# The modulation matrices' loads issued from GpSimd's queue in a twelve-phase transformer stack

## The chip, the cores and the metric

The kernel runs on one core of one Trainium2 chip. The metric is the device time of one execution in microseconds (us). The engines have short names in the profile: PE is TensorE, DVE is VectorE, ACT is ScalarE, POOL is GpSimd, SP is SyncE. Each has an instruction queue of its own and takes it in order: an instruction whose semaphore has not arrived holds up all that stand behind it on that engine. SPq and POOLq are the queue side of SP and POOL, on which DMAs are issued.

## What is computed

A sequence of 256 tokens by 1024 features, in float32, goes through two blocks of two layers. Each layer has three phases: a gated feed-forward net (FFN, inner width 2816), a mixer (a gated linear recurrence, a differential attention, and twice a sparse attention beside a spatial gate), and a second FFN. That makes twelve phases. Ahead of each phase the activations are normalised and modulated by rows that depend on a condition vector `c`:

```
mod = (silu(c) @ ada_w[l] + ada_b[l])            # nine rows of 1024 per layer: 3 phases x (shift, scale, gate)
h   = rmsnorm(x, g) * (1 + scale) + shift        # ahead of each phase
x   = x + gate * phase(h)                        # after each phase
```

Each row of `mod` needs a 1024x1024 slice of `ada_w`, 4 MB. These are the modulation matrices of this document.

## The kernel before

**Tiles.** Tokens are two tiles, T = 0 and 1, of 128. Every weight matrix is cut into chunks of up to four 128x512 blocks; half a chunk is loaded by one DMA of 512 KB into one of four `raw` buffers (`load_chunk`, line 194). ACT rounds it to `hi` (line 198), DVE subtracts to get `lo` (line 199), and three matmuls (`hi`, `lo` of the weight against `hi`, `lo` of the activation; two in part of the FFN) stand in for one float32 product. Eight pairs of `hi`, `lo` halves exist, so weights can be up to four chunks ahead of PE.

**Order.** The program is written out by hand as a long list: a queue of weight chunks with pieces of modulation work between them (`add_w`, `add_ada`; `ADA_SPAN` says over which chunks of a phase the pieces are spread). Every instruction has a place number in program order. `later(n)` adds n to it. A scheduler then lays out the queue of each engine from the instructions that are ready in its own reckoning, lower numbers first, and puts in the waits. On the chip each queue is then fixed.

**Modulation work.** For each of the 34 rows after the first two, `ada` takes an accumulator `acc` (two buffers) that POOL sets to zero (line 249), loads the bias `ada_b` into its first partition (SP, line 250), and then loads eight pieces `araw` of 128x1024 (512 KB each; two buffers, `ARAWS = 2`) with the DMA of line 258. DVE multiplies each by its column of silu(c) and adds it to `acc` (`accumulate`, line 265). With `ADA_LATER = 100` these accumulates have a late place number, so DVE takes them between its other work. A third `araw` can be loaded only when the first has been accumulated. When all eight are in, `row_sum` splits `acc` (lines 277, 278), adds the partitions up on PE (lines 282, 283) and writes the row; then the `acc` buffer is free.

**Norms.** At the end of each phase `residual` adds the gated output to `x` (lines 406, 407). `norm_half` then squares and sums on ACT (line 356) and makes the reciprocal root on POOL, by an add (line 358), an add (line 360) and a power (line 361). `pre` multiplies on DVE (line 379) and PE transposes the result (line 398) for the next phase's matmuls. The two tiles run three chunks apart (`LAG = 3`).

The first two rows, for phase 0, are loaded by other code (`ada_first`, line 335) into the weights' `raw` buffers; it is not touched.

Of the kernel before, what the change touches and what calls it, by code (L numbers as in the profile page):

```python
# [18 lines left out]
P = 128  # L19
D = 1024  # L20
# [61 lines left out]
class Net:  # L82
# [155 lines left out]
    def ada(self, piece):  # L238

        nc, A = self.nc, self.A  # L240
        st, q = piece
        b, l, j, kind = (st[k] for k in ("b", "l", "j", "kind"))
        sfx = "_2" if b else ""
        col = (j * 3 + kind) * D
        if q == 0:
            while len(self.row_stages) > 1:
                self.row_step()
            st["acc"] = self.t(self.tmp, [P, D], tag="acc", bufs=2)
            nc.gpsimd.memset(st["acc"], 0.0)  # L249
            nc.sync.dma_start(st["acc"][0:1, :], A["ada_b" + sfx][l:l + 1, col:col + D])  # L250
        if q == 2 and kind == 1:
            nc.sync.dma_start(self.S, A["norm_g" + sfx][l, j:j + 1, :].to_broadcast([P, D]))
        acc = st["acc"]
        for k in range(2 * q, 2 * q + 2):
            if len(self.araws) == ARAWS:
                self.accumulate()
            raw = self.araw()
            nc.sync.dma_start(raw, A["ada_w" + sfx][l][k * P:(k + 1) * P, col:col + D])
            self.araws.append((raw, k, acc, b, self.row_sum(b, l, j, kind, acc) if k == KD - 1 else None))

    def accumulate(self):
# [1161 lines left out]
def build(ctx, tc, A, which=None):  # L1423
# [15 lines left out]
    for i, (b, l, j, spec) in enumerate(ph):  # L1439
        ada = net.ada_pieces(b, l, j, 2)  # L1440
        if i + 1 < len(ph):
            b2, l2, j2, _ = ph[i + 1]
            ada += net.ada_pieces(b2, l2, j2, 1) + net.ada_pieces(b2, l2, j2, 0)
        if spec[0] == "ffn":
            cs = net.ffn_chunks(spec[1], spec[2], i == 0)
        elif spec[0] == "hgrn":
            cs = net.hgrn_chunks(A["a_w_in"][0], A["a_w_out"][0])
        elif spec[0] == "diff":
            cs = net.diff_chunks(A["b_w_in"][0], A["b_w_out"][0])
        else:  # L1450
            cs = net.nsa_chunks(A["mix_w_in_2"][l], A["proj_a_2"][l], A["proj_b_2"][l], A["w_out_2"][l])
        starts.append(len(net.chunks))
        done = 0
        for n, spec_ in enumerate(cs):
            if i == 0 and n == 3:
                net.queue.append(("f", second_half))
            if i + 1 < len(ph) and ph[i + 1][3][0] == "diff" and n == len(cs) // 2:
                net.queue.append(("f", diff_prep))
            net.add_w(*spec_)
            skip, tail = ADA_SPAN["first" if i == 0 else spec[0] if i + 1 < len(ph) else "last"]  # L1460
            want = max(0, n + 1 - skip) * len(ada) // (len(cs) - skip - tail)
            while done < min(want, len(ada)):
                net.add_ada(ada[done])
                done += 1
# [61 lines left out]
```

## Time and profile before

| what | value |
|---|---|
| time, median of 3 runs | 2245.66 us (2245.18 to 2247.92) |
| profiled execution: its own time | 2246.78 us |
| its span, first to last instruction | 2245.0 us |
| PE busy | 2201.0 us, 98% of the span |
| DVE busy | 1790.5 us, 80% |
| ACT busy | 1232.6 us, 55% |
| POOL busy | 112.8 us, 5% |
| bytes moved by DMA | 537.20 MB, mean 239 GB/s |

The span lies inside the execution's own time; 1.78 us lie around it. Busy time of PE includes matmuls that stream back to back. The difference between the span and PE's busy time, 44 us, is time in which PE did nothing.

### The profile page before, as it was taken

What the parts mean: (1) busy time and instruction counts of PE and PEld (TensorE: products, weight loads), DVE (VectorE), ACT (ScalarE), POOL (GpSimd) and SP (SyncE); (2) the same over time, 40 slices, a digit from 0 to 9 for tenths busy, and PEclk for the clock granted to TensorE, in tenths of its full rate; (3) what the DMA queues carried; (4) which work ended last, traced back from release to release, by engine and by line L of the source; (5) the groups of instructions that cost most, each with busy time, mean ns of one, the idle gap of its engine ahead of it and who ended that gap; (6) DMA issues with size and microseconds to landing.
All of it is one profiled execution on the core that took longest, in us unless ns stands there. A gap on an engine that the chain in (4) does not pass through costs nothing. (4 is left out here: it accounts for less than half of the span.)

```text
span 2245.0 us, 33267 instructions
## 1 busy us (share of the span) xinstructions
PE 2201.0 (98%) x12152; PEld 1820.6 (81%) x12152; DVE 1790.5 (80%) x2481; ACT 1232.6 (55%) x2182; POOL 112.8 (5%) x164
## 2 busy tenths in 40 slices
PE   8999999999999989999999999999999999999998
PEld 6887877888888767888888787788878878777886
DVE  7898987886878788887878778787877867887664
ACT  3664545564564586664565546466546644655653
POOL 1000101000000121000000000000000000000000
PEclk9999999999999999999999999999999999999999
DMA  9998865777877766877768787677777778755653
GB/s 299 303 310 286 286 207 185 268 256 245 265 230 263 235 225 202 286 247 253 255 224 267 232 256 227 195 254 229 262 229 255 254 247 266 244 173 179 187 171 111
DMA packets 264789, 537.20 MB, mean 239 GB/s; under 512 B 22083, under 2 KB 52619, under 8 KB 264625
## 3 DMA queue, kind: packets, MB, share of 16 engines
q1 hardware_dynamic: 264184, 534.67, 73.2%
q8 instruction: 95, 1.56, 0.3%
q14 instruction: 70, 0.57, 0.1%
q10 hardware_dynamic: 440, 0.40, 0.1%
HBM read 533.95 MB, written 1.05 MB: 238 GB/s over the span
## 5 line engine op out<-in xcount | busy, mean ns | idle before, releaser
L198 ACT ACTIVATE hi<-raw 128x1024 fp32r<-128x1024 f32 (+1 forms) x704 | 732.7, 1054 | 538.0 <-PE mm L457 329.9
L199 DVE TENSOR_TENSOR lo<-raw,hi 128x1024 fp32r<-128x1024 f32 (+1 forms) x704 | 845.1, 1214 | 221.0 <-ACT hi L198 217.2
L551 PE MATMUL mm<-hT,hi 128*128 128x512 f32 x2240 | 792.4, 398 | 0.0
L553 PE MATMUL mm<-hT,lo 128*128 128x256 f32 x2240 | 629.0, 281 | 0.0
L551 PEld LDWEIGHTS mm<-hT,hi 128*128 128x128 f32 x2240 | 420.8, 188 | 103.4
L553 PEld LDWEIGHTS mm<-hT,lo 128*128 128x128 f32 x2240 | 423.2, 189 | 1.3
L455 PE MATMUL mm<-hi,hT 128*128 128x512 f32 (+1 forms) x832 | 332.2, 399 | 1.5 <-ACT hT L385 1.1
L457 PE MATMUL mm<-hi,hT 128*128 128x512 f32 (+1 forms) x832 | 325.1, 392 | 0.5 <-DVE hT L387 0.5
L456 PE MATMUL mm<-lo,hT 128*128 128x512 f32 (+1 forms) x832 | 323.4, 389 | 0.0
L457 PE MATMUL mm<-hi,aT 128*128 128x512 f32 x704 | 278.3, 395 | 0.0
L455 PE MATMUL mm<-hi,aT 128*128 128x512 f32 x704 | 278.2, 395 | 0.0
L456 PE MATMUL mm<-lo,aT 128*128 128x512 f32 x704 | 277.8, 395 | 0.0
L265 DVE SCALAR_TENSOR_TENSOR acc<-araw,c_2s,acc 128x1024 f32<-128x1024 f32 x144 | 184.3, 1280 | 35.5 <-DMA araw<-ada_w 34.1
L455 PEld LDWEIGHTS mm<-hi,hT 128*128 128x128 f32 x832 | 156.9, 189 | 40.9 <-issue 8.6
L265 DVE SCALAR_TENSOR_TENSOR acc<-araw,cs,acc 128x1024 f32<-128x1024 f32 x128 | 163.8, 1280 | 31.2 <-DMA araw<-ada_w 30.6
L457 PEld LDWEIGHTS mm<-hi,hT 128*128 128x128 f32 x832 | 156.7, 188 | 34.5 <-DVE hT L387 1.2
L456 PEld LDWEIGHTS mm<-lo,hT 128*128 128x128 f32 x832 | 157.1, 189 | 29.9 <-issue 0.7
L456 PEld LDWEIGHTS mm<-lo,aT 128*128 128x128 f32 x704 | 132.6, 188 | 30.8
L457 PEld LDWEIGHTS mm<-hi,aT 128*128 128x128 f32 x704 | 132.6, 188 | 30.4
L455 PEld LDWEIGHTS mm<-hi,aT 128*128 128x128 f32 x704 | 132.6, 188 | 30.3
L536 ACT ACTIVATE aT<-uf 128x256 fp32r<-128x256 f32 x140 | 58.2, 416 | 92.7 <-DVE uf L534 92.7
L249 POOL MEMSET acc<- 128x1024 f32 x34 | 32.5, 956 | 1170.3 <-DVE accl L278 665.2
(287 smaller groups left out, 2182.4 us busy)
## 6 DMA issues: line engine op xcount, KB each, us to landing
araw<-ada_w SPq DMA_DIRECT2D x272, 512.0 KB
raw<-ffn_wi SPq DMA_DIRECT2D x160, 512.0 KB
raw<-ffn_w_in SPq DMA_DIRECT2D x160, 512.0 KB
raw<-ffn_wo SPq DMA_DIRECT2D x88, 512.0 KB
raw<-ffn_w_out SPq DMA_DIRECT2D x88, 512.0 KB
raw<-mix_w_in SPq DMA_DIRECT2D x64, 512.0 KB
raw<-a_w_in SPq DMA_DIRECT2D x32, 512.0 KB
raw<-b_w_in SPq DMA_DIRECT2D x24, 512.0 KB
```

Of the source, the lines that this page charges most:

```text
L198: nc.scalar.activation(hi[:, :n, :w], r, AF.Copy)
L199: nc.vector.tensor_sub(lo[:, :n, :w], r, hi[:, :n, :w].bitcast(F32))
L249: nc.gpsimd.memset(st["acc"], 0.0)
L265: self.nc.vector.scalar_tensor_tensor(acc, raw, self.cs[b][:, k:k + 1], acc, op0=OP.mult, op1=OP.add)
L455: nc.tensor.matmul(ps, lhsT=h, rhs=hi, start=start and i == 0, stop=False)
L456: nc.tensor.matmul(ps, lhsT=h, rhs=lo, start=False, stop=False)
L457: nc.tensor.matmul(ps, lhsT=l, rhs=hi, start=False, stop=stop and i == c.nk - 1)
L536: nc.scalar.activation(hi, u, AF.Copy)
L551: nc.tensor.matmul(ps[f], lhsT=c.hi(k)[:, fs], rhs=x, start=kh == 0 and k == 0, stop=False, skip_group_check=True)
L553: nc.tensor.matmul(ps[f][:, 0:256], lhsT=c.lo(k)[:, fs], rhs=x[:, 0:256], start=False, stop=kh == 1 and k == 3, skip_group_check=True)
```

## The change

The DMA that loads a piece of a modulation matrix is issued by GpSimd in place of SyncE. Source, destination, size and buffers stay as they are. The bias load (line 250), the load of the norm's gain (line 252), `ada_first` and all weight loads stay on SyncE.

```
--- before.py
+++ after.py
@@ -255,7 +255,7 @@
             if len(self.araws) == ARAWS:
                 self.accumulate()
             raw = self.araw()
-            nc.sync.dma_start(raw, A["ada_w" + sfx][l][k * P:(k + 1) * P, col:col + D])
+            nc.gpsimd.dma_start(raw, A["ada_w" + sfx][l][k * P:(k + 1) * P, col:col + D])
             self.araws.append((raw, k, acc, b, self.row_sum(b, l, j, kind, acc) if k == KD - 1 else None))
 
     def accumulate(self):
```

## Rows read from the trace of the kernel before

**Rows 1.** The page: busy time by engine; DMA share in 40 equal slices.
```profile
PE 2201.0 (98%) x12152; PEld 1820.6 (81%) x12152; DVE 1790.5 (80%) x2481; ACT 1232.6 (55%) x2182; POOL 112.8 (5%) x164
...
DMA  9998865777877766877768787677777778755653
```

**Rows 2.** Windows: stretch, length, busy us by engine (count), clock, DMA share, GB/s.
```profile
0.00:60.00 60.00, 54.11 (x207) 38.05 (x208) 42.82 (x60) 21.90 (x32) 7.30 (x16) 1.00 0.91 299
60.00:200.00 140.00, 139.51 (x718) 117.58 (x717) 125.97 (x171) 78.16 (x125) 2.46 (x3) 1.00 0.90 304
200.00:400.00 200.00, 189.94 (x1853) 162.20 (x1852) 169.95 (x213) 106.95 (x175) 19.86 (x27) 0.99 0.72 234
400.00:700.00 300.00, 299.06 (x1583) 254.41 (x1583) 243.33 (x322) 171.61 (x282) 8.12 (x11) 1.00 0.77 253
700.00:900.00 200.00, 190.25 (x909) 151.06 (x908) 163.88 (x244) 128.30 (x361) 31.53 (x39) 0.98 0.70 227
900.00:2000.00 1100.00, 1091.37 (x5697) 900.18 (x5696) 889.01 (x1264) 601.04 (x1016) 37.74 (x56) 1.00 0.76 244
...
2200.00:2245.00 45.00, 37.63 (x162) 30.09 (x161) 19.40 (x23) 13.44 (x20) 2.46 (x6) 0.94 0.28 93
```

**Rows 3.** Waits of PE: total us, times, longest us.
```profile
PE tr L398 <- DVE xs L379: 9.0, 17, 1.0
...
PE tr L398 <- ACT hi L198: 4.1, 6, 0.7
```

**Rows 4.** Waits of SP's queue, same columns.
```profile
SPq L194 <- DVE lo L199: 877.1, 484, 8.9
SPq L258 <- DVE acc L265: 234.9, 155, 6.0
...
SPq L258 <- DMA araw<-ada_w: 62.4, 43, 4.4
SPq L250 <- POOL acc L249: 49.4, 27, 3.6
```

**Rows 5.** Line 258: issue time, ns min/median/max, first and last start.
```profile
L258 SPq DMA_DIRECT2D araw<-ada_w x272: 327/341/1771, 62.6 to 1997.8; - x136
```

**Rows 6.** POOL's lines, same columns; the last is its longest instruction.
```profile
L249 POOL MEMSET acc<- x34: 952/956/962, 40.1 to 1962.6; 128x1024 f32 x34
L360 POOL TENSOR_TENSOR ss<-ss x26: 189/492/989, 15.5 to 2240.0; 128x1 f32<-128x1 f32 x26
L361 POOL TENSOR_TENSOR ss<-ss,mhalf x26: 551/570/1062, 16.2 to 2240.2; 128x1 f32<-128x1 f32 x26
L670 POOL TENSOR_TENSOR qst<-qst,mhalf x4: 1661/1664/2203, 785.4 to 829.3; 128x8 f32<-128x8 f32 x4
```

**Rows 7.** DVE's two kinds with the most work around the change, same columns.
```profile
L199 DVE TENSOR_TENSOR lo<-raw,hi x704: 741/1218/1228, 21.5 to 2223.4; 128x1024 fp32r<-128x1024 f32 x174, 128x560 fp32r<-128x560 f32 x2
L265 DVE SCALAR_TENSOR_TENSOR acc<-araw,c_2s,acc x144: 1265/1279/1286, 904.9 to 2003.0; 128x1024 f32<-128x1024 f32 x144
```

**Rows 8.** Windows of line 265 alone: stretch, length, DVE busy us (count), clock, DMA.
```profile
60.00:200.00 140.00, 38.40 (x30) 1.00 0.90 304
```

**Rows 9.** Waits of DVE: total us, times, longest us.
```profile
DVE acc L265 <- DMA araw<-ada_w: 64.7, 60, 2.8
...
DVE xs L379 <- POOL ss L361: 15.5, 22, 1.3
```

**Rows 10.** SP's queue in order of time, 0 to 130 us: start, us, issues.
```profile
62.58 0.46 SPq L258 DMA_DIRECT2D araw<-ada_w  x1
...
102.83 0.32 SPq L250 DMA_DIRECT2D acc<-ada_b  x1
```

**Rows 11.** POOL in order of time, 0 to 330 us: the second accumulator's memset.
```profile
47.10 0.96 POOL L249 MEMSET acc<- 128x1024 f32 x1 [6.00 <-PE tr L341]
```

**Rows 12.** The chain that ended last, in order of time: start, us, piece.
```profile
1969.95 3.33 DMA araw<-ada_w
...
2054.58 0.84 POOL ss L360
```

More of the change, by code (lines that the diff above doesn't have):

```diff
@@ L257, in ada @@
             raw = self.araw()
-            nc.sync.dma_start(raw, A["ada_w" + sfx][l][k * P:(k + 1) * P, col:col + D])
+            nc.gpsimd.dma_start(raw, A["ada_w" + sfx][l][k * P:(k + 1) * P, col:col + D])
             self.araws.append((raw, k, acc, b, self.row_sum(b, l, j, kind, acc) if k == KD - 1 else None))
```

## The prediction

> **What bounds the kernel now.** I read the busy times first, then the windows, the waits of PE, the queue of SP, POOL's lines, and last the chain that ended last.
>
> PE is busy 98% of the span [rows 1], and in the long stretches nearly all of it: 139.5 of 140 us from 60 to 200, 299.1 of 300 from 400 to 700, 1091.4 of 1100 from 900 to 2000 [rows 2]. There the end is set by the count of matmuls, and no load can shorten it. What is left to gain or lose is PE's idle time, 2245.0 - 2201.0 = 44 us. By stretch: 5.9 us in the first 60 (nothing to multiply yet), 10.1 from 200 to 400 and 9.8 from 700 to 900 (the linear recurrence and the differential attention, chains of small steps), 8.6 over the 1100 us from 900 to 2000, 7.4 in the tail [rows 2], and some 2 in the rest. The largest single reason that PE waits is the end of the norms: 17 waits for line 379, 9.0 us in all [rows 3]. Line 379 in turn waits for POOL's power 22 times, 15.5 us [rows 9]. So POOL, 5% busy [rows 1], stands on the path at the phase boundaries. One of its adds lies in the chain that ended last, at 2054.58, 0.84 us [rows 12].
>
> Weights are not late. SP waits 877 us at line 194, but for DVE to free a `raw` buffer [rows 4], which means that loads run ahead as far as buffers let them. PE's waits that trace to the split of weights (line 198) are 4.1 us [rows 3].
>
> **SP is relieved.** It loses 272 issues at 0.341 us [rows 5], 93 us of queue time, and the two longest waits in front of them, 234.9 us for a free `araw` and 62.4 us for a transfer [rows 4]. Behind each such wait stood weight loads. They can now go earlier, but still wait for `raw` buffers, and PE waited only 4.1 us for the split. I cost this at nothing: the cover is the lookahead of eight weight halves. The bound of the gain is that 4.1 us.
>
> The Trainium skill, "DMA: Bandwidth & Descriptors", section "Issuing engines are not separate DMA queues", says that all issuing engines feed the same 16 DMA engines, so that a second issuer only saves the first one's issue time. By that rule alone the sum would be the time before, with SP's 93 us saved off the path; the row of line 258 agrees that this time exists, and no row before can show the interleaving.
>
> **DVE may wait less.** DVE waited 64.7 us in 60 waits for an `araw` to land [rows 9], because the issue stood behind weight loads in SP. With a queue of its own a piece can be issued when its buffer is free. Little of this is on the path: the chain that ended last passes through an `araw` transfer for 3.33 us, one piece of note [rows 12]. Between nothing and 9.0 us (all of PE's waits for line 379 [rows 3], if every one came of a DVE queue held up by a late piece), I take half of the one piece that the chain shows: -1.7 us.
>
> **The start.** Before, the first piece is issued at 62.58 us, because SP has weights ahead of it [rows 10]. On POOL nothing stands in front: both `araw` buffers are empty from the start. POOL does run ahead where it can: the memset of the second accumulator runs at 47.10 us [rows 11], 56 us before SP loads that accumulator's bias at 102.83 [rows 10]. So the first two pieces may be issued in the first microseconds. They are 2 x 0.524 MB = 1.05 MB, and the first 60 us already move 299 GB/s at a DMA share of 0.91 [rows 2], so 1.05 / 0.299 = 3.5 us of other loads come later, while PE waits for its first inputs. A delay there is not won back, since PE is full from 60 us on. Below: nothing, if the scheduler leaves the two at their old place or they fall behind what PE needs. I take half, +1.7 us.
>
> **POOL's issues.** No row shows a DMA issued by POOL. From both sides: SP's issue, 0.341 us [rows 5], and POOL's longest instruction, 2.203 us [rows 6]. I take the row that it is nearest to, a POOL instruction that writes SBUF over 128 partitions and reads none, the memset at 0.956 us [rows 6]. 272 x 0.956 = 260 us, 11.6% of the span, beside the 112.8 us of now: POOL has room. What it costs is that a norm's add or power (0.492 and 0.570 us [rows 6]) finds an issue running: 0.116 x 0.956 / 2 = 0.06 us each time; with 2.203 us a piece, 0.27 x 1.1 = 0.3 us.
>
> **POOL's waits.** The waits for a free `araw` go along to POOL. An accumulate has a late place number, so POOL's head will often be a load that waits for DVE. Behind it stand the adds and powers of the norms, and the memsets; for the memset waits SP's bias load, today already 49.4 us in 27 waits [rows 4], and behind that the weights. SP met these waits late and still waited 234.9 / 155 = 1.5 us, up to 6.0 [rows 4]. Loads come every (1997.8 - 62.6) / 271 = 7.1 us [rows 5]. So a waiting load is at the head for at least 1.5 / 7.1 = 0.21 of the time. I take that share of the 17 places where PE waits for line 379 [rows 3] to lose 1.5 us each, 0.32 on average. With the 0.06 above: 17 x 0.38 = 6.4 us. Below: nothing, if the scheduled order puts each norm ahead of the loads. Above: all 17 at the 6.0 us of the longest wait, 102 us, which needs the worst order at every boundary; all 17 at the mean, 26 us, is a bound that could happen.
>
> **The sum.** 2246.8 (the profiled execution's time, 2245.0 of it span) + 6.4 + 1.7 - 1.7 = 2253.2. That execution lies 1.1 us above the median of the runs, 2245.66, so in terms of the median 2252.1: I forecast 2252 us, slower by 0.28%.
>
> **Rivals.** *No change that can be measured.* A difference under 0.2%, 4.5 us, can't be told from none: 2241.2 to 2250.2. It comes if the scheduled order of POOL puts the norms ahead of waiting loads, or the loads simply keep their old places: then 2245.7 plus or minus the two small terms, 2244 to 2249. For it: POOL is 5% busy and DVE frees buffers every few microseconds. Against it: 17 places, each of which needs only 0.26 us (4.5 / 17) to decide.
>
> *Faster.* One mechanism: DVE's in-order queue no longer stands at an accumulate whose piece is late, so the norms' multiplies and the recurrence's steps behind it go earlier. It decides from half of PE's 9.0 us on [rows 3]: 2241 to 2237, when all 9.0 go. For it: 64.7 us of such waits on an engine that is 80% busy. Against: the chain crosses only one of note.
>
> *DVE is held up by POOL.* If an instruction of POOL kept DVE's two-input operations waiting for its length, then from 60 to 200 us, where DVE is busy 126.0 of 140 [rows 2], the 30 pieces [rows 8] at 0.956 us add 28.7: 154.7 us of work in 140, 14.7 too much, for which PE would wait: 2260. Against: over 34 memsets and 26 norms on POOL, lines 199 and 265 never ran longer than 1.228 and 1.286 us against medians of 1.218 and 1.279 [rows 7], and no memset was stretched (952 to 962 ns [rows 6]). POOL's adds, which read, were (189 to 989 ns). The Trainium skill, "SBUF — State Buffer", section "SBUF: two separate sides", warns the other way round: descriptors of a DMA issued from GpSimd are made by its cores, which can't write them while DVE holds the shared port in a 2-port mode. By that the issues would be stretched rather than DVE; the trace agrees in so far as no write of POOL was stretched by these two lines; no run before shows a DMA of POOL's. The price of stretched issues is that of the bound above, 2.2 us each: 17 x (0.32 + 0.3) = 10.5, for 2256.
>
> *POOL's queue blocks at most boundaries*: 26 us of waits, 2272; behind late memsets SP's bias load and the weights go late too.
>
> **Chances and range.** The forecast, slower by 0.2 to 0.6% (2250.2 to 2260, with the stretched issues in it): 0.37. No change: 0.34. Faster: 0.18. Blocked at most boundaries, or DVE held up: 0.11, from 2260 on. So faster 0.18, same 0.34, slower 0.48. The likeliest alone lies between 2250 and 2260. The range for 8 in 10 reaches over no change into the faster case and up into the blocked one: 2239.5 to 2275.
>
> **What the profile after would show.** Right: line 258 on POOLq, 272 times, near 1 us; SP's waits at 258 gone; the first `araw` in the first 20 us, and the first matmul with weights 1 to 3 us later than before; POOL's wait list led by line 258 waiting for DVE at 265; PE's waits for line 379 grown from 9.0 to about 15 us; DVE's waits for landing pieces down from 64.7. Wrong: if the PE waits for line 379 stay, the waits in POOL's queue don't meet the norms; if PE's busy time rather than its idle time grows, the cause is none of these; if issues on POOL take several microseconds each, POOL is a bound of its own, and the time is far above the range. What would break the forecast most easily is the order that the scheduler gives all queues with a new owner for 272 DMAs: it can move every small wait of the 44 us by chance.

## The result, and the profile after

| | before | after |
|---|---|---|
| time, median (lowest to highest) | 2245.42 us (2244.57 to 2247.92) | 2282.01 us (2280.07 to 2285.76) |
| span of the profiled execution | 2245.0 us | 2279.6 us |
| PE busy, and idle in the span | 2201.0, 44.0 us | 2207.5, 72.1 us |

The ratio is 1.0158, 95% interval 1.0146 to 1.0170: 1.6% slower, 36.6 us. The direction was forecast, the size was not: 2252 us, with a range that ended at 2275. Of the 34.6 us by which the span grew, 28.1 are new idle time of PE and 6.5 new busy time.

From the page of the kernel after: busy times, one DMA queue, the chain that ended last by engine and by line, the DMA issues with their median time from issue to landing.

```profile
PE 2207.5 (97%) x12152; PEld 1821.4 (80%) x12152; DVE 1788.1 (78%) x2481; ACT 1228.7 (54%) x2184; POOL 263.6 (12%) x436
...
q0 software_dynamic: 39168, 142.62, 19.0%
...
PE mm L551 19%; PE mm L455 10%; PE mm L457 10%; PE mm L456 10%; PE mm L553 10%; DMA araw<-ada_w 8%; DVE lo L199 3%; PE tr L398 2%; ACT hi L198 2%; DVE acc L265 1%; DMA raw<-ada_w 1%; DMA raw<-ffn_wi 1%; DMA raw<-mix_w_in 1%; DVE xs L406 0%;
...
araw<-ada_w POOLq DMA_DIRECT2D x272, 512.0 KB, 4.7
```

The pieces have a queue of their own (q0), and POOL has room. Transfers of pieces are now 8% of the chain that ended last. The chain of before goes back only to 1668.85 us, the last quarter of the span, and holds one such transfer, of 3.33 us [rows 12]; over the same last part the chain of after holds 13.

Line 258 after, on POOL: ns min/median/max of one issue, first and last start.

```profile
L258 POOL DMA_DIRECT2D araw<-ada_w x272: 530/530/778, 1.7 to 2019.8; - x136
```

Waits of PE after (total us, times, longest us), to be held against [rows 3]:

```profile
PE tr L398 <- DVE w L922: 8.9, 4, 5.5
PE tr L398 <- DVE xs L379: 7.6, 15, 0.8
PE tr L398 <- DVE sst L1340: 7.5, 2, 4.6
...
PE mm L551 <- DVE gf L521: 4.4, 3, 1.6
...
PE tr L283 <- DVE accl L278: 3.5, 4, 2.6
```

The ends of the norms (line 379) cost no more than before. What grew is a handful of long waits for DVE. Line 922 turns q and k of the differential attention; PE waited for it before too, but for shorter times:

```profile
PE tr L398 <- DVE w L922: 5.3, 3, 2.2
```

Line 1340 is the softmax of the sparse attention, lines 521 and 278 belong to the FFN and to the row sums. For lines 1340 and 521 the profile before lists no wait of PE, for 278 one of 0.5 us.

Waits of DVE after, to be held against [rows 9], and below them those of POOL and of SP [rows 4]:

```profile
DVE acc L265 <- DMA araw<-ada_w: 119.0, 88, 5.5
...
DVE xs L379 <- POOL ss L361: 15.0, 22, 1.3
```
```profile
POOL araw L258 <- DVE acc L265: 812.4, 227, 12.1
```
```profile
SPq L194 <- DVE lo L199: 1224.8, 487, 18.3
...
SPq L250 <- POOL acc L249: 65.5, 30, 9.5
```

SP is rid of line 258. It waits longer than before for `raw` buffers (877.1 us before), and 65.5 us for the memset ahead of the bias load (49.4 before). POOL stands at line 258 for 812 us in SP's place. DVE's waits for landing pieces have nearly doubled, from 64.7 us in 60 waits to 119.0 in 88, where the forecast had them fall.

**Where the time went.** PE runs its 12152 instructions in both kernels, nearly all in the same order, so the start of the n-th can be compared. How much later it starts than before, gained within each stretch (times are those of before; two columns of kernels explained below):

| stretch of before, us | after | old order on POOL | norms ahead |
|---|---|---|---|
| 0 to 59, start | 3.8 | 4.3 | 5.1 |
| 59 to 220, first FFN | 9.6 | -0.9 | -0.9 |
| 220 to 767 | -0.7 | 0.2 | 2.3 |
| 767 to 897, differential attention | 6.7 | 6.7 | 2.9 |
| 897 to 1406 | 0.5 | 0.8 | 0.4 |
| 1406 to 1442, end of a sparse attention | 6.3 | 0.0 | 0.0 |
| 1442 to 1991 | 2.5 | 1.6 | 0.8 |
| 1991 to 2030, end of the second one | 4.2 | 0.0 | 0.0 |
| sum, to the last matmul | 33.1 | 12.6 | 10.6 |
| behind the last matmul | 1.6 | 1.6 | 1.6 |

The last row is the end of the program. The last matmul starts 7.8 us ahead of the end of the span where SyncE issues all loads (before, and experiment 2), and 9.3 us in the kernel after and in experiment 1. What grew is the longest of GpSimd's three drains (`DRAIN`) at line 1522, the end of the program. Before and after, ns min/median/max of one:

```profile
L1522 POOLq DRAIN  x3: 34/78/657, 2240.2 to 2244.7; - x3
L1522 POOLq DRAIN  x3: 40/102/5577, 2273.3 to 2279.4; - x3
```

**One place closely.** At the first end of a sparse attention, before and after in order of time (start, us, engine, line; in brackets the idle time before it and what ended it). Before:

```profile
1410.78 0.69 DVE L1333 TENSOR_REDUCE sst<-mm 128x2 f32<-128x512 f32 x1 [2.51 <-PE mm L1324]
...
1418.86 1.28 DVE L265 SCALAR_TENSOR_TENSOR acc<-araw,c_2s,acc 128x1024 f32<-128x1024 f32 x1
```

After:

```profile
1425.06 0.53 POOL L258 DMA_DIRECT2D araw<-ada_w  x1 [8.14 <-DVE acc L265]
...
1433.65 1.28 DVE L265 SCALAR_TENSOR_TENSOR acc<-araw,c_2s,acc 128x1024 f32<-128x1024 f32 x1 [5.53 <-DMA araw<-ada_w]
1434.85 0.68 DVE L1333 TENSOR_REDUCE sst<-mm 128x2 f32<-128x512 f32 x1
...
1440.86 1.04 PE L398 MATMUL tr<-ident,ring 128*128 128x128 f32 x4 [4.60 <-DVE sst L1340]
...
1442.26 2.08 PE L1324 MATMUL mm<-kall,qT 64*128 64x512 f32 x4
```

The piece's transfer in the chain that ended last (start, us):

```profile
1425.06 8.49 DMA araw<-ada_w
```

Before, the softmax's reduction (line 1333) runs as soon as its matmuls are done, and the accumulate follows 8 us later. After, an accumulate stands ahead of the reduction in DVE's queue. Its piece isn't there, DVE waits 5.53 us, and PE then stands 4.60 us for the softmax. Two things meet here: DVE's queue has another order, and the transfer took 8.49 us where the median is 4.7, at a DMA share of 0.98 from 1425.06 to 1433.56 us. At the median, by an estimate from these two numbers, it would have landed 3.8 us earlier. The program, sizes and buffers are the same, but with another owner for 272 DMAs the scheduler laid out the queues anew: in DVE's, 534 of 2481 places hold another kind of instruction than before, in PE's 189 of 12152. POOL's own 164 instructions keep their order.

### The profile page after: what moved, and what is told of

Same layout as the page of the kernel before. It is cut to its first block, busy times and chain, and to the rows that moved or that the text cites. A ratio compares the mean times of both kernels' runs of the same rounds, so it can differ in the third digit from the quotient of the medians.

```text
span 2279.6 us, 33403 instructions
## 1 busy us (share of the span) xinstructions
PE 2207.5 (97%) x12152; PEld 1821.4 (80%) x12152; DVE 1788.1 (78%) x2481; ACT 1228.7 (54%) x2184; POOL 263.6 (12%) x436
## 4 chain that ended last, share of the span: by engine, by line
PE 63%; DMA 10%; issue 10%; DVE 10%; ACT 4%; POOL 2%; POOLq 0%; DVEq 0%; ACTq 0%
PE mm L551 19%; PE mm L455 10%; PE mm L457 10%; PE mm L456 10%; PE mm L553 10%; DMA araw<-ada_w 8%; DVE lo L199 3%; PE tr L398 2%; ACT hi L198 2%; DVE acc L265 1%; DMA raw<-ada_w 1%; DMA raw<-ffn_wi 1%; DMA raw<-mix_w_in 1%; DVE xs L406 0%; PE tr L283 0%
## 5 line engine op out<-in xcount | busy, mean ns | idle before, releaser
L258 POOL DMA_DIRECT2D araw<-ada_w x272 | 147.2, 541 | 930.9 <-DVE acc L265 812.4
```

The costliest lines, as they stand in the source:

```text
L258: nc.gpsimd.dma_start(raw, A["ada_w" + sfx][l][k * P:(k + 1) * P, col:col + D])
```

## Experiments

In ten of the fourteen kernels an order is written down: between neighbours of a queue stands an edge that the scheduler must keep and that becomes no wait on the chip (the kernel after, and the one of experiment 8 with that order written down, both have 33403 instructions). So the order of one kernel can be run with the issuing engine of the other. The loads of line 258 are left free within their engine's queue (in experiment 5 GpSimd's whole queue, in experiment 3 all but DVE's).

```
+        row = [here[k] for k in names if k in here]
...
+        for prev, ins in zip(row, row[1:]):
+            tc.add_manual_dep(ins, prev.name,
+                              mybir.DependencyInfo(mybir.DependencyClass.NoSync, mybir.DependencyReason.DATA),
+                              reason="pin")
```

Medians below stand beside the kernel before on the same chip: 2245.4 us in experiments 1, 2 and 8, 2246.0 in 3 to 7 and 9, 2247.3 in 10.

**1. The old order, loads on GpSimd.** The kernel after, all queues in the order of before.

> GpSimd issues the 272 loads, but the order of every queue (PE, DVE, ACT, SP, POOL) is pinned to that of the kernel before; only the loads themselves are placed freely on POOL. Theory 'order' (most of the 36 us comes of where the scheduler put DVE's accumulates): 2245.4 plus the 4.5 us of the start, as the two first loads still run ahead: 2247 to 2253. Theory 'queue' (loads through POOL's queue land later or wait longer, whatever the order): 2270 to 2282, with DVE's wait for landing pieces near the 119 us of after.

2261.85 us, ratio 1.0072 (1.0057 to 1.0087): 16.4 us slower than before, and 20 faster than after. So the order is worth more than half of the loss, and the rest needs no new order. Waits of DVE and PE in it:

```profile
DVE acc L265 <- DMA araw<-ada_w: 77.1, 63, 3.2
```
```profile
PE tr L398 <- DVE xs L379: 9.4, 17, 1.0
PE tr L398 <- DVE w L922: 6.4, 2, 4.9
```

**2. The new order, loads on SyncE.** The kernel before, all queues in the order of after.

> SyncE issues all loads as in the kernel before, but the order of every queue is pinned to that of the kernel after; only the loads of line 258 are placed freely on SP. Theory 'order': slow although GpSimd issues nothing, 2268 to 2285 (the start without its 4.5 us, weights behind loads that wait a little later). Theory 'queue': 2243 to 2250.

2294.33 us, 1.0213 (1.0196 to 1.0230): the new order is slow with no DMA on GpSimd at all. Its waits of DVE and of PE:

```profile
DVE acc L265 <- DMA araw<-ada_w: 131.8, 71, 6.4
```
```profile
PE mm L551 <- DVE gf L521: 15.6, 6, 4.0
```

It is slower than after by 12 us, so issuing from GpSimd is the better of the two in this order. The two halves of the loss don't simply add, and the 49 us are not the price of the order alone. In the new order DVE takes its first accumulate before 61 us. In the kernel after, that piece is loaded from 1.75 us on. Here SyncE issues the load only at 56.97 us, behind weights; DVE waits for it and PE for DVE, so that some 8 us are lost at this one place:

```profile
56.97 8.09 SPq L258 DMA_DIRECT2D araw<-ada_w  x3
...
63.42 1.28 DVE L265 SCALAR_TENSOR_TENSOR acc<-araw,cs,acc 128x1024 f32<-128x1024 f32 x1 [6.90 <-issue]
...
65.89 0.80 PE L456 MATMUL mm<-lo,hT 128*128 128x512 f32 x1 [5.77 <-DVE lo L199]
```

**3. DVE's queue alone in the old order**, the others laid out by the scheduler.

```
+def pin(nc, tc, engines=("DVE",)):
```

> All 272 loads on POOL; only DVE's queue is pinned to the order of before, the others are laid out freely. Theory 'accumulates' (the places of line 265 in DVE's queue are what the new order lost by): 2258 to 2266, like the run with all queues pinned. Rival (the orders of PE, ACT and SP matter): 2270 to 2282.

2263.79 us, 1.0091 (1.0066 to 1.0115): with DVE's order alone 18 of the 36 us are back, nearly all that the five queues together gave. Its runs go from 2260.81 to 2272.40, so the two can't be told apart.

**4. Another place number.**

```
-ADA_LATER = 100
+ADA_LATER = 400
```

> The kernel after with ADA_LATER = 400 for 100, so that accumulates have a later place number and DVE takes them behind more of its other work. Theory 'accumulates': DVE stands less at late pieces, and the time falls by 5 to 15 us, to 2267 to 2277. Rival (the place number hardly matters, as accumulates are laid out by when the scheduler holds them to be ready): 2278 to 2286.

2281.44 us, 1.0160 (1.0144 to 1.0175). Nothing changed: DVE's queue is that of after but for two places, so a later place number doesn't bring the old order back.

**5. Six accumulates moved.** The order of after, but in DVE's queue three accumulates at each of the two ends of a sparse attention stand behind the softmax (each bracket names three accumulates and the scaling, line 1344, that they go behind).

```
+LATER = [(("I-14840", "I-14962", "I-14965"), "I-13763"), (("I-20909", "I-21123", "I-21124"), "I-19215")]
```

> After's order in every queue but for six accumulates in DVE's queue, three near 1433 us and three near 2018 us of after's trace: they stand behind the scaling of the softmax (line 1344) instead of ahead of its reduction (line 1333). Theory (DVE's accumulates were laid out ahead of work that PE waits for): PE's waits for line 1340, 4.6 and 3.7 us there, go, and so does what the two places cost against the kernel before, 6.3 and 5.2 us in steps of PE's instructions: 11 us less than after, near 2271. Rival (the pieces that DVE waits for are late anyway, and the wait only goes to another place): 2280 to 2284.

2279.84 us, 1.0153 (1.0136 to 1.0170), at the lower end of what the rival gave: the theory is refuted. The two places still lost 5.7 and 3.2 us. In order of time:

```profile
1433.66 2.60 DVE L265 SCALAR_TENSOR_TENSOR acc<-araw,c_2s,acc 128x1024 f32<-128x1024 f32 x2
...
1435.24 0.53 POOL L258 DMA_DIRECT2D araw<-ada_w  x1 [12.19 <-DVE acc L265]
...
1440.74 1.29 DVE L265 SCALAR_TENSOR_TENSOR acc<-araw,c_2s,acc 128x1024 f32<-128x1024 f32 x1 [4.48 <-DMA araw<-ada_w]
...
1443.67 0.69 DVE L1333 TENSOR_REDUCE sst<-mm 128x2 f32<-128x512 f32 x1
...
1447.96 0.63 PE L398 MATMUL tr<-ident,ring 128*128 128x128 f32 x4 [3.30 <-DVE sst L1340]
```

This shows one thing that makes a piece late. Two accumulates run, each frees a buffer, the load for the third goes out at once (1435.24) and its accumulate can start 5.5 us later. In between DVE has nothing that stands ahead of it, so it waits 4.48 us, now in front of the next softmax. Moving an accumulate back moves its successor's load back as well.

So I counted, for each accumulate, DVE's own work since the end of the accumulate two before it, the one that frees its buffer. Where that is less than a load's round trip (from the freeing accumulate's end to landing, 5.0 us by the median of after), DVE mostly waits: at 78 of the 109 such places in after. A transfer takes 3.5 to 10.3 us there, so the count is no sharp line. For the kernels with three buffers (experiment 6) it is the accumulate three before.

| kernel | under 5 us of work | DVE idle in front of accumulates, us |
|---|---|---|
| before | 84 of 270 | 64.5 |
| old order on POOL | 83 | 78.1 |
| after | 109 | 124.1 |
| new order on SP | 109 | 133.4 |
| before, 3 `araw` | 4 of 269 | 18.3 |
| after, 3 `araw` | 10 | 30.1 |

**6. A third `araw` buffer**, in both kernels, paid for with one `raw` buffer, since both don't fit.

```
-RAWS = 4
-ARAWS = 2
+RAWS = 3
+ARAWS = 3
```

> The changed kernel with three araw buffers, paid for with one of the four raw buffers. Read against before_33 alone. Theory (DVE stands at pieces that are issued too late, because a load waits in POOL's queue for one of two buffers): a third buffer lets each load be issued one piece earlier, DVE's waits for pieces fall from 119 us to half or less, and the ratio to before_33 comes down from 1.016 to 1.008 or less. Rival (what costs is the order of the queues, whatever the buffers): the ratio stays 1.013 or more.

> The kernel before with three araw and three raw buffers, the base for after_33. Both theories: slower than the kernel before by what the fourth raw buffer is worth, between nothing and 40 us; DVE's waits for pieces below the 64.7 us of before.

2308.79 us against 2268.65: before with the third buffer is 1.0101 (1.0086 to 1.0116) of before, after with it 1.0277 (1.0262 to 1.0293), so 1.8% lie between them, no less than without. DVE's waits for pieces, of after_33 and then of before_33:

```profile
DVE acc L265 <- DMA araw<-ada_w: 28.7, 21, 3.7
```
```profile
DVE acc L265 <- DMA araw<-ada_w: 16.4, 17, 3.0
```

The waits went as expected and the loss did not. This refutes late pieces as the one cause: where they are nearly gone, the change costs 40 us in a third layout. The order hurts there in other ways: PE waits 7.8 us for the softmax's scaling (line 1344), for which it waited in no place of before_33, while its waits for line 379 hardly differ (19.8 and 17.9 us).

**7. A rule in place of a written order.** Each load has an edge to the weight load that stands ahead of it in the program.

```
+            load = nc.gpsimd.dma_start(raw, A["ada_w" + sfx][l][k * P:(k + 1) * P, col:col + D])
+            self.tc.add_manual_dep(load.ins, self.weight.ins.name,
+                                   mybir.DependencyInfo(mybir.DependencyClass.NoSync, mybir.DependencyReason.DATA),
+                                   reason="behind the weights")
```

> The changed kernel with one more rule for the scheduler: a load of line 258 isn't laid out before the weight load that stands ahead of it in the program. It adds no wait on the chip, and no order is written down. Theory (half of the loss is the order that the scheduler makes when it lets GpSimd's loads run ahead of the weights): the first araw goes back behind the first weights, the start costs at most 1 us, and the time is that of the kernels with the old order, 2255 to 2266. Rival (any new order that isn't the old one costs as much): 2276 to 2290.

2308.1 us, 1.0271 (1.0249 to 1.0293), a miss for both. The first loads did go back, to 48.98 us, yet it is a fourth layout, and the slowest with two buffers. Only 67 of its accumulates have under 5 us of work, and DVE waits 74.4 us for pieces. What PE waits for most in it is the multiply of the spatial gate beside the sparse attention (lines are shifted by 3):

```profile
PE tr L401 <- DVE m L1188: 15.0, 3, 7.4
```

**8. The start.** Two kernels keep the first two loads behind the first memset of line 249, in the old order and in the new.

```
...
+            if len(self.held) < 2:
+                self.tc.keep_in_program_order(load)
+                self.held.append(load.ins.name)
```

> As the run with the order of before, and the first two loads stand on POOL behind the memset of their accumulator, which ran at 40 us in the kernel before. Theory 'start' (the two loads that run ahead cost 4.5 us): 4 to 5 us less than the run without the hold. With theory 'order' that is 2243 to 2249, no change from before; under 2241 if the free SP queue is worth something. Theory 'queue': 2265 to 2278.

> The kernel after with the order of every queue pinned to its own, except that the first two loads stand on POOL behind the memset of their accumulator. Theory 'start': the first matmul with weights returns from 30.4 to about 25.9 us, and the time falls by 4 to 5 us, to 2277 to 2278. Rival (the delay of the start is hidden by what is late anyway in the next 160 us): 2280 to 2283.

2261.32 us, 1.0071 (1.0056 to 1.0086), and 2277.81, 1.0147 (1.0125 to 1.0169). In the new order the median falls into the range of the theory, but its runs go from 2273.79 to 2283.56, and the profiled one (2281.67) was 6.2 us late at 59 us, later than without the edit, so that the start won the 4 us is not shown. In the old order nothing was won. The first matmul with weights starts at 26.60 instead of 31.32 us (25.88 before), but by 59 us PE is as late as without the edit. In order of time (lines shifted by 1 to 4):

```profile
41.40 1.33 POOL L259 DMA_DIRECT2D araw<-ada_w  x2
...
52.73 1.38 PE L402 MATMUL tr<-ident,xs 128*128 128x128 f32 x8 [2.09 <-DVE xs L383]
```

The pieces now load at 41 us, and a norm's end is late instead. At both places tried, 1.75 and 41 us, 1 MB more pushed out something that PE needs; the whole stretch moves at a DMA share of 0.91 [rows 2].

**9. Some loads back on SyncE**, in the old order: the first two, and then those of the differential attention's phase as well (24; for them `st["sp"]` is true).

```
-            nc.gpsimd.dma_start(raw, A["ada_w" + sfx][l][k * P:(k + 1) * P, col:col + D])
+            self.pieces += 1
+            (nc.sync if self.pieces <= 2 or st["sp"] else nc.gpsimd).dma_start(
+                raw, A["ada_w" + sfx][l][k * P:(k + 1) * P, col:col + D])
```

> Every queue in the order of before; the first two of the 272 loads on SP in their old place, the other 270 on POOL. Theory 'start' (two loads within the first 60 us delay inputs by 4 us, wherever POOL issues them in that time): 4 us under the run with the order of before, 2256 to 2259, and no delay at 60 us. Rival (DMA of the first 60 us is not the cause): 2260 to 2264.

> As the run with two loads on SP, and the 24 loads whose pieces belong to the differential attention's phase also on SP; 246 on POOL. Theory 'norms behind loads' (on POOL the norms of queries and keys stand behind a load that waits for DVE: 6 to 8 us lost between 780 and 900 us): 2249 to 2252. Rival (that loss is DVE waiting for pieces that land late, on either queue): 2255 to 2259.

2259.71 us, 1.0059 (1.0044 to 1.0075), and 2261.38, 1.0066 (1.0051 to 1.0081). The first misses its theory's 2259 by 0.7 us and lies 2 us under experiment 1, within what the runs scatter. At 59 us the two are 2.4 and 1.1 us late, where experiment 1 was 4.3: the delay of the start shrinks when its loads leave it, and the total hardly follows. With the attention's loads on SyncE its stretch lost 1.2 us instead of 6.7, but in that profile PE lost 3.9 us near 1030 and 4.0 near 1919, where the old order on POOL had lost nothing and 0.9. The total didn't fall: a miss. In front of the first of them (lines shifted by 2 and 3):

```profile
1007.33 0.53 POOL L260 DMA_DIRECT2D araw<-ada_w  x1 [4.94 <-DVE acc L268]
...
1014.30 1.28 DVE L268 SCALAR_TENSOR_TENSOR acc<-araw,c_2s,acc 128x1024 f32<-128x1024 f32 x1 [3.42 <-DMA araw<-ada_w]
```

A crowded accumulate again, here in an FFN, with a load that took 6.5 us to land. Why it meets PE in this execution and not in the others of the same order stays open.

**10. The norms of q and k ahead of the loads.** In the old order on POOL, at 790 us (experiment 1):

```profile
790.66 0.53 POOL L258 DMA_DIRECT2D araw<-ada_w  x1 [3.88 <-DVE acc L265]
...
791.59 1.67 POOL L670 TENSOR_TENSOR qst<-qst,mhalf 128x8 f32<-128x8 f32 x1
793.29 0.69 DVE L914 TENSOR_TENSOR w<-mm,qst 128x512 f32<-128x512 f32 x1 [2.94 <-POOL qst L670]
...
797.08 1.08 PE L398 MATMUL tr<-ident,w 128*128 128x128 f32 x4 [4.87 <-DVE w L922]
```

A load waits 3.88 us for its buffer, the norm behind it waits along, then DVE 2.94 us for the norm, then PE 4.87 us. The edit lays four loads behind the norms that follow them; the second kernel also issues the first two loads from SyncE.

```
+BEHIND = [("I-7957", "I-7729"), ("I-8023", "I-7889"), ("I-8185", "I-8148"), ("I-9273", "I-8555")]
```

> All 272 loads on GpSimd, every queue in the order of before, but in GpSimd's queue four loads of the differential attention stand behind the q/k or head norm that they stood in front of (those that in the kernel without this edit ran at 790.7, 810.0, 832.2 and 870.8 us and had waited 3.9, 3.1, 0.2 and 3.3 us for a buffer). DVE, ACT, PE and SP keep their queues. Theory (about half of what is left in the old order is norms held behind a waiting load): the stretch from 767 to 897 us of before, which lost 6.7 us in steps of PE's instructions, loses 2 or less, and the time falls from 2261.9 to 2255 to 2258. Rival (the load goes later instead, and DVE stands at its piece): 2260 to 2264.

> The same edit, and the first two loads issued by SyncE at their old place, so that the start is that of before. Theory (start and norms are the two named costs of GpSimd's issue, and the rest is small): 2250 to 2254. Rival (what is taken away at one place comes back at others, as it did when 26 loads were on SyncE): 2257 to 2263.

2262.09 us, 1.0065 (1.0053 to 1.0077), and 2255.93, 1.0046 (1.0029 to 1.0064; runs from 2252.18 to 2264.66). The same place in the first of them:

```profile
791.27 0.25 POOL L667 TENSOR_SCALAR qst<-qst 128x8 f32<-128x8 f32 x1 [1.46 <-ACT junk L906]
791.60 1.67 POOL L670 TENSOR_TENSOR qst<-qst,mhalf 128x8 f32<-128x8 f32 x1
...
793.24 0.61 POOL L258 DMA_DIRECT2D araw<-ada_w  x1
793.31 0.69 DVE L914 TENSOR_TENSOR w<-mm,qst 128x512 f32<-128x512 f32 x1 [0.41 <-PE mm L457]
...
797.09 0.63 PE L398 MATMUL tr<-ident,w 128*128 128x128 f32 x4 [1.99 <-DVE w L922]
```

The norm no longer waits for the load, PE's wait falls from 4.87 to 1.99 us, and the stretch lost 2.9 us instead of 6.7. In the medians this is 14.8 us over before instead of 16.4, within what the runs scatter and within the rival's range: the place is shown, its worth in the time is not. With both edits 8.6 us remain. In the profiled execution the steps sum to 5.4 us, of which 0.4 up to 59 us, and 1.4 more lie behind the last matmul. That is half of experiment 1's loss, and still 2 us above the range that the theory gave.

No kernel tried beats the one before.

## Why the prediction was wrong, step by step

**The step that failed** is the sum itself: it priced GpSimd's issues and waits as if each queue kept its order. The new order stood there only as what "would break the forecast most easily", without a price or a chance: the sum put it at nothing. By experiments 1 and 3 it is 18 to 20 of the 36.6 us, and by experiment 2 it costs on SyncE too. The terms that the sum did have were short as well: 6.4 us in all, where experiment 1 with the old order measured 16.4. The rows that could have warned are [rows 9] and [rows 3]: DVE already waited 64.7 us for pieces of which little met PE, so the old order held these waits off the path, and a new one need not.

**"DVE may wait less", -1.7 us**, had the wrong sign. Its size was read from a chain that covers only the last quarter of the span, so "one piece of note" told nothing of the first 1668 us. In the old order the forecast gain is there: in front of accumulates with 6 us of work or more between, DVE's idle time falls from 13.3 to 2.1 us, since their loads no longer stand behind weights. But the 101 crowded ones are bound by the round trip, and theirs rises from 51.2 to 76.0 us. By the median an accumulate's end is followed by the next load 0.30 us later on POOL and 0.03 on SP, and the issue takes 0.53 us where SP's took 0.341 [rows 5]. Together that is 0.46 us a round trip; over the 63 waits of experiment 1 it would be 29 us, an estimate from these rows that is near the 24.8 by which the crowded waits grew. In the new order 129 are that crowded, with 122.1 us.

**The start, +1.7 us**, was the right mechanism and too small. The two loads were issued at 1.75 us, and PE waited for a transfer of the first two rows' own matrices (line 340) before any weights came:

```profile
1.75 1.33 POOL L258 DMA_DIRECT2D araw<-ada_w  x2
...
14.30 2.05 PE L340 MATMUL tr<-raw,cs_rows 128*128 128x512 f32 x2 [3.08 <-DMA raw<-ada_w]
```

The first matmul with weights came 4.55 us later (30.43 against 25.88), and 3.8 us were left at 59 us. The bound of 3.5 us for both pieces was the value to take, not half of it. Experiment 8 shows that a place 40 us later was not free either.

**POOL's waits, 6.4 us**, was the right mechanism at the wrong place. The ends of the phases did not suffer: PE's waits for line 379 are 7.6 us after and 9.4 in the old order, 9.0 before, and DVE's waits for POOL's power hardly moved (15.5 before, 15.0 after). What stood behind waiting loads were the norms of q and k on POOL. That stretch lost 6.7 us in both orders, and in the old order 3.8 of them went with experiment 10.

**POOL's issues** took 0.53 us, not 0.956: 147.2 us in all. **DVE held up by POOL** is refuted: lines 265 and 199 ran at most 1.305 and 1.243 us against 1.286 and 1.228 [rows 7]. No issue took over 0.778 us either. The Trainium skill, "SBUF — State Buffer", section "SBUF: two separate sides", warns that GpSimd can't write a DMA's descriptors while DVE runs an operation in a 2-port mode. In the issue times this does not show here; for the time to landing (3.5 to 10.3 us) the trace before has no counterpart. The Trainium skill, "DMA: Bandwidth & Descriptors", section "Issuing engines are not separate DMA queues", says that DMAs of all issuing engines run on the same 16 DMA engines. The trace agrees: the first 60 us move 299 GB/s after as before, whoever issues. By that rule alone the time would have stayed. It says nothing of queue order, where more than half of the loss came from.

**SP relieved at nothing** was right: no matmul of the kernel after starts earlier than its counterpart before.

**The end of the program** had no term either. It took 1.6 us more in the profile after, as in experiments 1 and 10 with all loads on GpSimd.

**What stays open**: which trait of the new order costs what. Crowding explains DVE's waits, and one place was followed to PE, but experiments 5 to 7 each removed a trait and not the loss. Open too is the share of slow transfers in the late pieces, which no run tells apart from the order. Of GpSimd's half, some 8 us lie neither at the start nor at the four norms. The end of the program is 1.6 of them; the rest is spread over the stretches at some 2 us or less each. One small wait recurs: at a row sum (884 us of before, where PE had no such wait) PE stands 1.0 to 2.1 us for line 277 in all seven kernels with DVE's old order and loads on GpSimd. In experiment 1:

```profile
893.29 0.50 PE L282 MATMUL tr<-acch,ones 128*128 128x512 f32 x1 [2.10 <-ACT acch L277]
```

## What to carry to other kernels

Moving a DMA to another engine changes the scheduler's input, so compare the order of all queues before pricing the move; where it differs, run the new engine in the old order and the old engine in the new. With two buffers a load can't be issued before the consumer two back is done: count the consumer engine's own work between the two against the round trip, and let nothing that the bounding engine needs stand behind a consumer with less. On an engine with small steps of the critical path, lay a load that will wait for its buffer behind the step, not ahead of it. What these last two rules are worth in time no run here shows: the waits moved, the medians hardly did.

## What the runs showed of the hardware

TensorE's clock made the long waits dearer: its mean over the span was 0.997 before and 0.994 after. After PE had worked 0.26 us in 4.86, the granted clock of the next 3.5 us was 0.52, the lower of its two levels (1.2 of 2.4 GHz), and line 1324's four matmuls took 2.08 us (1.13 at 1409.62 us of before, where the clock was 1.00). Windows of after: stretch, length, busy us by engine, clock, DMA share, GB/s.

```profile
1436.00:1440.86 4.86, 0.26 (x3) 0.03 (x1) 3.93 (x10) 3.94 (x11) 0.98 (x2) 1.00 0.67 217
1440.86:1444.40 3.54, 3.54 (x11) 1.57 (x12) 3.54 (x6) 2.75 (x4) 0.07 (x1) 0.52 0.62 174
```

The stretch with the wait of 4.60 us lost 6.3 us, and over the span PE's busy time grew by 6.5 us with the same 12152 instructions. How much of either is the clock was not separated.
